# Four regroupings in a one-core hybrid decoder layer: decay rows, a transpose, a weight split and the last products

## The chip, the cores and the metric

The kernel runs on one core of one Trainium2 chip. The metric is device time in microseconds of the whole program, the median of several executions. One execution was also recorded by the hardware profiler; all positions below ("at 995.82") are microseconds from the start of that recording's span. The engines are TensorE (PE: matmuls; PEld: its weight loads), VectorE (DVE), ScalarE (ACT), GpSimd (POOL) and SyncE (SP, which only asks for transfers here). ACT and POOL also ask for transfers; the profile calls the queues SPq, ACTq and POOLq.

## The reference

One decoder layer on 512 tokens of width 1024, all in float32, cut to its steps:

```python
x = x + 0.5 * swiglu(rms_norm(x, norm_ffn1_w), ffn1_w_in, ffn1_w_out)      # D_FF = 2816
x = x + hybrid_mixer(rms_norm(x, norm_mix_w), ...)   # SSD heads beside differential attention
x = x + memory_cross_attention(rms_norm(x, norm_cross_w), rms_norm(mem, norm_mem_w), ...)
x = x + 0.5 * swiglu(rms_norm(x, norm_ffn2_w), ffn2_w_in, ffn2_w_out)
return rms_norm(x, norm_final_w)

def swiglu(h, w_in, w_out):
    gate, up = jnp.split(h @ w_in, 2, axis=-1)
    return (jax.nn.silu(gate) * up) @ w_out

# in hybrid_mixer, for the 16 SSD heads in 4 groups, chunks of 128 tokens:
la_cum = jnp.cumsum(la, axis=2)
seg = la_cum[:, :, :, None] - la_cum[:, :, None, :]
decay = jnp.exp(jnp.where(causal[None, None, :, :, None, None], seg, -jnp.inf))
cb = jnp.einsum('bclgn,bcsgn->bclsg', cc, bc)
y_diag = jnp.einsum('bclsg,bclsgr,bcsgrp->bclgrp', cb, decay, xdt)
...
y_off = jnp.einsum('bclgn,bcgrpn,bclgr->bclgrp', cc, prev, jnp.exp(la_cum))
```

## The kernel before

The activations live as eight tiles `x[0..7]` of 128 channels by 512 tokens. Each weight tile (128 by 1024, 512 KB) is loaded by SP into `wr`, and split into a rounded high part `wh` (ACT, line 153) and a remainder `wl` (DVE, line 154); a product is three matmuls (high by high, low by high, high by low). There are six `wr` buffers and three each of `wh` and `wl`.

The order in which work is written out comes from `Order`: dense generators (the projections, one after the other) and chains (side work such as attention heads) that are resumed when a running estimate of TensorE's time, `od.t`, reaches their due time. SP and POOL execute their instructions in exactly that written order. On PE, ACT and DVE a compiler's planner decides the order from its own estimates of when each instruction will be ready, with what is written earlier going first among ready ones; on the chip each engine then works strictly through the order it was given.

The places that the change touches:

- FFN1 (`ffn1`): a first part with plain projections (`NPLAIN`), then "quads" (`quad`, `add_product`, line 238): blocked products by a scheme with seven products instead of eight, called 11, S1, S2, 12, S3, S4 and 22 by the half-token operands they use. Their operands `s31` and `s24` are sums of token halves of channel pairs, made by `block_sums`. The product 11 goes into the bank `qa`, S1 into `qe`, and `qa` is copied to `qb` by ACT. With `fresh=True` (the first quad of each FFN) the last channel pair is left to the end: `qa` for three pairs, `qe` for three pairs, then the last pair of each. In FFN1 a quad's T1 weight is summed by an accumulating transfer that POOL asks for (line 246).
- SSD groups (`group`): `decays(j)` asks POOL's queue for rows of the cumulative log decay (`cum_d`, in DRAM) for two heads, broadcast over 128 partitions, into the single-buffered tiles `gate` (j=0) and `th` (j=1) (line 820). ACT turns them into decays (lines 879 to 882), DVE masks them (line 883), PE multiplies (`py`); `pf` takes the carried state, `st` (lines 859 to 867).
- `block_sums_in_dram`: a chain that adds weight blocks for FFN2 in DRAM: ACT asks for a copy, POOL four jobs later for the accumulating transfer (line 1143). The list `hold` keeps POOL's part back while a group is between its start and its second half.
- The last projection of cross attention (`out_proj` with `upd_2`) finishes `x[o]` for o = 0..7 and prepares FFN2's operands. `turn` transposes all eight `x` tiles in place through PSUM tiles `pxf` (PE, line 148, then ACT, line 1116), 30 time units after the last one, inside FFN2's first quads.
- FFN2's last output products (`out_blocks` with `last`): `update` adds a PSUM bank to a 128-token row block of `x` (DVE, line 1183), and `final` makes the final norm: a Square with row sum on ACT (1247), `fv` on DVE (1250/1252), the gain on DVE (1253), the power −1/2 on POOL (1258), the scaling of both halves on ACT (1259, 1262; the last half on DVE, 1264), and the stores.

Of the kernel before, what the change touches and what calls it, by code (L numbers as in the profile page):

```python
# [13 lines left out]
AF = mybir.ActivationFunctionType  # L14
# [3 lines left out]
P = 128  # L18
# [80 lines left out]
def body(tc, a, dbg=None):  # L99
# [28 lines left out]
    def acc(s, shape=(P, T)):  # L128
        return acc_p.tile(list(shape), F32, tag="acc", name=nm(s))
# [8 lines left out]
    last, start, last_sum, recent, hold = [], [], [], [], []  # L138
    V, S, G = nc.vector, nc.scalar, nc.gpsimd
    od = Order()  # L140

# [113 lines left out]
    def quad(xs, src, ready, fresh=False):  # L255

        b12, b11, b22, b21 = src[0], src[1], src[2], src[3]
        m1 = raw_w(b11)
        if ready:
            t, t2, m2, m7, m3 = raw_w(ready[0]), raw_w(ready[1]), raw_w(b21), raw_w(b12, b22), raw_w(b22)
            t4 = m2
        else:
            t, m3, m2, m7 = raw_w(b12, b11), raw_w(b22), raw_w(b21), raw_w(b12, b22)
            t2 = t4 = t
        a_ps = acc("qa")  # L270
        e_ps = acc("qe")
        b_ps = acc("qb")
        if fresh:

            n = len(xs)
            w1, w5 = split_w(m1), split_w(t)
            yield from add_product(a_ps, w1, xs, "11", True, range(n - 1))
            yield from add_product(e_ps, w5, xs, S1, True, range(n - 1))
            yield from add_product(a_ps, w1, xs, "11", False, range(n - 1, n))
            S.activation(b_ps, a_ps, AF.Copy)  # L280
            yield from add_product(e_ps, w5, xs, S1, False, range(n - 1, n))
        else:
            yield from add_product(a_ps, split_w(m1), xs, "11", True)
            S.activation(b_ps, a_ps, AF.Copy)
            yield from add_product(e_ps, split_w(t), xs, S1, True)
        p5 = s2("p5")
        S.activation(p5, e_ps, AF.Copy)
        if not ready:
            V.tensor_tensor(t2, t, m3, ALU.add)
        yield from add_product(b_ps, split_w(t2), xs, S2, False)  # L290
        if not ready:
            V.tensor_tensor(t4, t2, m2, ALU.add)
        u2 = s2("u2")
        S.activation(u2, b_ps, AF.Copy)
        V.tensor_tensor(e_ps, e_ps, u2, ALU.subtract)
        yield from add_product(a_ps, split_w(m2), xs, "12", False)
# [180 lines left out]
    def ffn1(h, wa, on_final, at_out):  # L477
        row4, xs = None, []
        wq, plain = iter(a["f1q"]), a["f1i"]
        for ti, (_, nf) in enumerate(THIRDS):  # L480
            g = []
            nq = nf // 2
            if ti == 0:
                for made in ffn_first(h, wa):
                    if made is None:
                        yield
                    else:
                        g.append(split("g", gated(*made, st1.row)))
                row4 = s2("row4")
                V.tensor_scalar(row4, st1.row, 0.25, None, ALU.mult)  # L490
                for n in range(NPLAIN - 2):
                    pg, pu = acc("pg"), acc("pu")
                    yield from proj(pg, load_w(plain[n][0]), h)
                    yield from proj(pu, load_w(plain[n][1]), h)
                    g.append(split("g", gated(pg, pu, st1.row)))
                    xs.append(block_sums(2 * n, C_FFN1, of_halves(h[2 * n], h[2 * n + 1])))
                nq -= NPLAIN // 2
            yield from ffn_quads(xs, wq, st1, nq, whole_tiles(g), BY_TILE, None, ti == 0)
            at_out(ti)
            for o in range(KT):  # L500
# [102 lines left out]
    def steps(pdt):  # L603
# [42 lines left out]
        ct_sb = s2("ct_sb", shape=(64, P))  # L646
        V.tensor_copy(ct_sb, pct)
        nc.gpsimd.dma_start(cum_d, ct_sb)
        dump("cum", cum)


# [145 lines left out]
    def group_dense(g):  # L797
# [6 lines left out]
        for j in range(2):  # L804
            ps = acc("pz")
            yield from proj(ps, load_w(a["wz"][2 * g + j]), h)
            zs.append(silu2(ps))

    def group(g, bt, ct, xs, zs):
        hsl = slice(4 * g, 4 * g + 4)  # L810

        def by_head(t):
            return t.rearrange("p c (h e) -> p c h e", e=64)

        def decays(j):
            rs, both = [], s4(("gate", "th")[j])
            for hh in range(2):
                r = both[:, 2 * hh : 2 * hh + 2].rearrange("p a (b c) -> p (a b) c", c=P)
                hd = 4 * g + 2 * j + hh
                nc.gpsimd.dma_start(r, bass.AP(cum_d.tensor, cum_d.offset + hd * P, [[0, P], [16 * P, 4], [1, P]]))  # L820
                rs.append(r)
            return rs

        hold.append(g)

        pcb = aux("pcb", (P, 4, P))
        for c in range(4):
# [40 lines left out]
            st.append(sc)  # L868
            yield W["gs"] if c < 2 else W["gt"]
        yz = []  # L870
        rs = decays(0)
        for j in range(2):
            py = aux("py")
            e2 = s2("e2")
            for hh in range(2):
# [9 lines left out]
            for c in range(1, 4):  # L885
                mm(pf[:, c * P : (c + 1) * P], st[c - 1][:, j * P : (j + 1) * P], ct[:, c * P : (c + 1) * P], True, True)
            yield W["gd"]
            if j == 1:
                hold.remove(g)
            for c in range(4):  # L890
                for hh in range(2):
                    pp = slice(64 * hh, 64 * hh + 64)
                    mm(py[pp, c * P : (c + 1) * P], xdt[c // 2][:, c % 2, (2 * j + hh) * 64 : (2 * j + hh + 1) * 64], rs[hh][:, c], True, True)
            if j == 0:
                rs = decays(1)
            dsk = dskh[:, 2 * g + j : 2 * g + j + 1]
            V.scalar_tensor_tensor(e2[:, P:], pf[:, P:], 0.5, e2[:, P:], ALU.mult, ALU.mult)
            y = s2("y")
# [209 lines left out]
    def turn():  # L1108

        for n in range(2):  # L1110
            pt = [aux("pxf") for _ in range(4)]
            for tb in range(4):
                for j in range(4):
                    transpose(pt[tb][:, j * P : (j + 1) * P], x[4 * n + j][:, tb * P : (tb + 1) * P])
            for tb in range(4):
                S.activation(x[4 * n + tb], pt[tb], AF.Copy)
                yield 4.0


    isum = [[dram.tile([P, D], F32, name=f"isum{g}{t}") for t in range(2)] for g in range(NF // 2)]  # L1120
# [2 lines left out]
    def block_sums_in_dram():  # L1123
# [22 lines left out]
    def out_blocks(c, g, col4, last):  # L1146

# [34 lines left out]
        def update(tb, half_, src):  # L1182
            V.scalar_tensor_tensor(x[4 * half_ + tb], src, col4[:, tb : tb + 1], x[4 * half_ + tb], ALU.mult, ALU.add)  # L1183
            if last is not None:
                last(tb, half_)

        bank = [acc, aux]
        a_ps = [bank[t]("oa") for t in range(2)]
# [32 lines left out]
        if last is None:  # L1221
# [16 lines left out]
    def ffn2():  # L1238
        wq, in_sums = iter(a["f2q"]), iter(isum)
        col4, gain = None, []  # L1240

        sq = {}

        def final(tb, n):

            xt, ss, junk = x[4 * n + tb], small("fss", 1), s2("junk")
            S.activation(junk, xt, AF.Square, accum_out=ss)
# [6 lines left out]
            if tb not in sq:  # L1254
                sq[tb] = v
                return
            rr = small("frr", 1)
            G.tensor_tensor(rr, v, mhalf[:, 0:1], ALU.pow)  # L1258
            S.activation(x[tb], x[tb], AF.Copy, scale=rr)  # L1259
            nc.sync.dma_start(a["out"][tb][:, :T], x[tb])  # L1260
            if tb < 3:
# [5 lines left out]
        for c, (_, nf) in enumerate(THIRDS):  # L1267
# [10 lines left out]
            yield from out_blocks(c, g, col4, final if at_end else None)  # L1278

    od.add(ffn2())  # L1280
    od.run()
    ctx.close()
# [89 lines left out]
```

## Time and profile before

| | us |
|---|---|
| median of 3 runs | 1337.62 |
| lowest, highest | 1336.28, 1339.88 |
| profiled execution, its time | 1339.54 |
| profiled execution, span from first to last instruction | 1337.8 |
| PE busy | 1310.7 (98%) |
| DVE busy | 975.6 (73%) |
| ACT busy | 667.4 (50%) |
| POOL busy | 129.9 (10%) |
| mean granted TensorE clock | 0.992 |

How to read it: the span is the profiled execution's own; 1.74 us of that execution's time lie around the span. A matmul counts as busy until its modelled end, so that consecutive matmuls overlap and "busy" does not mean that the array is at its peak. "Idle before, releaser" in a row is the time in which that engine did nothing ahead of the instruction, and the event that ended it.

### The profile page before, as it was taken

What the parts mean: (1) busy time and instruction counts of PE and PEld (TensorE: products, weight loads), DVE (VectorE), ACT (ScalarE), POOL (GpSimd) and SP (SyncE); (2) the same over time, 40 slices, a digit from 0 to 9 for tenths busy, and PEclk for the clock granted to TensorE, in tenths of its full rate; (3) what the DMA queues carried; (4) which work ended last, traced back from release to release, by engine and by line L of the source; (5) the groups of instructions that cost most, each with busy time, mean ns of one, the idle gap of its engine ahead of it and who ended that gap; (6) DMA issues with size and microseconds to landing.
All of it is one profiled execution on the core that took longest, in us unless ns stands there. A gap on an engine that the chain in (4) does not pass through costs nothing. (4 is left out here: it accounts for less than half of the span.)

```text
span 1337.8 us, 20033 instructions
## 1 busy us (share of the span) xinstructions
PE 1310.7 (98%) x7769; PEld 1139.7 (85%) x7769; DVE 975.6 (73%) x1535; ACT 667.4 (50%) x1127; POOL 129.9 (10%) x155
## 2 busy tenths in 40 slices
PE   9999999999999999999999999999999999999996
PEld 7888999899887778877778887888889989998995
DVE  6875688477886586557847877656687886887787
ACT  6442455154554465346545546434445654655556
POOL 0000001000020111200112032010002101000000
PEclk9999999999999999999989999999999999999998
DMA  7434577546394636674475557776268977665653
GB/s 269 118 103 126 129 204 237 144 115 190 125 280 125 174 82 106 194 209 111 113 146 154 107 132 220 200 202 160 67 216 210 223 227 208 183 194 183 182 172 118
DMA packets 65695, 222.71 MB, mean 166 GB/s; under 512 B 8424, under 2 KB 10960, under 8 KB 65248
## 3 DMA queue, kind: packets, MB, share of 16 engines
q1 hardware_dynamic: 47088, 150.30, 34.7%
q0 software_dynamic: 14208, 47.79, 20.5%
q10 hardware_dynamic: 4304, 23.33, 5.3%
q8 instruction: 61, 1.00, 0.3%
q14 instruction: 34, 0.28, 0.1%
HBM read 219.24 MB, written 50.91 MB: 202 GB/s over the span
## 5 line engine op out<-in xcount | busy, mean ns | idle before, releaser
L153 ACT ACTIVATE wh<-wr 128x1024 fp32r<-128x1024 f32 (+2 forms) x311 | 317.2, 1022 | 400.9 <-issue 72.9
L154 DVE TENSOR_TENSOR wl<-wr,wh 128x1024 fp32r<-128x1024 f32 (+2 forms) x311 | 366.3, 1178 | 122.0 <-ACT wh L153 120.1
L144 PE MATMUL po<-gh,wh 128*128 128x512 f32 x176 | 68.8, 392 | 0.0
L144 PE MATMUL po<-gl,wh 128*128 128x512 f32 x176 | 68.5, 390 | 0.0
L144 PE MATMUL po<-gh,wl 128*128 128x512 f32 x176 | 68.4, 389 | 0.0
L238 PE MATMUL qa<-hmh,wh 128*128 128x256 f32 x216 | 61.7, 286 | 0.2 <-ACT wh L153 0.2
L238 PE MATMUL qa<-hml,wh 128*128 128x256 f32 x216 | 61.5, 285 | 0.0
L238 PE MATMUL qa<-hmh,wl 128*128 128x256 f32 x216 | 61.4, 284 | 0.0
L144 PE MATMUL pxbc<-hnh,wh 128*128 128x512 f32 x128 | 52.3, 409 | 0.0
L144 PE MATMUL pxbc<-hnh,wl 128*128 128x512 f32 x128 | 50.4, 394 | 0.0
L144 PE MATMUL pxbc<-hnl,wh 128*128 128x512 f32 x128 | 50.1, 391 | 0.0
L238 PE MATMUL qe<-s31h,wh 128*128 128x256 f32 x152 | 43.9, 289 | 4.9 <-ACT s31h L153 3.2
L696 ACT ACTIVATE ec<-ec,mn 128x512 f32<-128x512 f32 (+3 forms) x64 | 35.4, 555 | 26.3 <-DVE mn L695 26.3
L238 PE MATMUL qe<-s31h,wl 128*128 128x256 f32 x152 | 43.6, 287 | 0.8 <-DVE wl L154 0.8
L504 DVE TENSOR_TENSOR upd<-po,row 128x512 f32<-128x512 f32 x24 | 16.6, 690 | 38.1 <-PE po L144 38.0
L238 PE MATMUL qb<-s24h,wh 128*128 128x256 f32 x152 | 43.8, 288 | 0.2
L238 PE MATMUL qb<-s24l,wh 128*128 128x256 f32 x152 | 43.8, 288 | 0.0
L238 PE MATMUL qb<-s24h,wl 128*128 128x256 f32 x152 | 43.8, 288 | 0.0
L238 PE MATMUL qe<-s31l,wh 128*128 128x256 f32 x152 | 43.4, 286 | 0.0
L238 PE MATMUL qe<-s24h,wh 128*128 128x256 f32 x152 | 43.0, 283 | 0.0
L238 PE MATMUL qe<-s24l,wh 128*128 128x256 f32 x152 | 43.0, 283 | 0.0
L238 PE MATMUL qe<-s24h,wl 128*128 128x256 f32 x152 | 43.0, 283 | 0.0
(448 smaller groups left out, 4097.2 us busy)
## 6 DMA issues: line engine op xcount, KB each, us to landing
wr<-in_f2q SPq DMA_DIRECT2D x44, 512.0 KB, 4.4
wr<-in_f1q SPq DMA_DIRECT2D x40, 512.0 KB, 4.2
isum<-in_f2q ACTq DMA_DIRECT2D x22, 512.0 KB, 4.8
wr<-isum SPq DMA_DIRECT2D x22, 512.0 KB, 4.4
wsum<-in_f2b ACTq DMA_DIRECT2D x20, 512.0 KB, 5.5
wr<-wsum SPq DMA_DIRECT2D x20, 512.0 KB, 4.4
wr<-in_f1q POOLq DMA_DIRECT2D x16, 512.0 KB, 6.5
wr<-in_f1o SPq DMA_DIRECT2D x16, 512.0 KB, 3.9
```

Source lines behind the costliest of these rows:

```text
L144: nc.tensor.matmul(out, w, x, start=start, stop=stop)
L153: S.activation(hi, src, AF.Copy),
L154: V.tensor_tensor(lo, src, hi.bitcast(F32), ALU.subtract),
L238: nc.tensor.matmul(out, a_[:, wc], b_, start=first and f == 0 and kp == 0 and j == 0, stop=kp == n - 1 and j == 2, skip_group_check=True)
L504: V.tensor_tensor(upd, po, row4, ALU.mult)
L696: S.activation(ec[:, :n], ec[:, :n], AF.Exp, bias=mn, scale=-1.0, accum_out=sm[c][:, i : i + 1])
```

## The change

Four things are regrouped; nothing is computed differently.

1. FFN1: the block sums of a channel pair are written ahead of that round's two plain projections instead of behind them, and FFN1's first quad is no longer `fresh`. In every quad the T1 weight is split (`w5`) ahead of the copy of `qa` to `qb` in the written order.
2. SSD: `decays(0, j)` is asked for as soon as `cum_d` is written, and `decays(g + 1, j)` directly behind group g's `py` products of the same j. `hold` is gone; the accumulating jobs are 9 instead of 8 time units apart.
3. `turn` is cut in two: tiles 0 to 3 from o = 4 of the last projection on, tiles 4 to 7 between that projection and FFN2. Its 16 transposes each are ordered by source tile.
4. In FFN2's last output products, `final` is cut into `norm` and `store`, and a new function `at_last` writes them out in an order of its own, inside a region in which DVE and ACT keep the written order among the region's instructions.

```diff
 def quad(xs, src, ready, fresh=False):
+        w1, w5 = split_w(m1), split_w(t)
         if fresh:
             n = len(xs)
-            w1, w5 = split_w(m1), split_w(t)
...
         else:
-            yield from add_product(a_ps, split_w(m1), xs, "11", True)
+            yield from add_product(a_ps, w1, xs, "11", True)
             S.activation(b_ps, a_ps, AF.Copy)
-            yield from add_product(e_ps, split_w(t), xs, S1, True)
+            yield from add_product(e_ps, w5, xs, S1, True)
...
 def ffn1(h, wa, on_final, at_out):
                 for n in range(NPLAIN - 2):
+                    xs.append(block_sums(2 * n, C_FFN1, of_halves(h[2 * n], h[2 * n + 1])))
                     pg, pu = acc("pg"), acc("pu")
                     yield from proj(pg, load_w(plain[n][0]), h)
                     yield from proj(pu, load_w(plain[n][1]), h)
                     g.append(split("g", gated(pg, pu, st1.row)))
-                    xs.append(block_sums(2 * n, C_FFN1, of_halves(h[2 * n], h[2 * n + 1])))
...
-            yield from ffn_quads(xs, wq, st1, nq, whole_tiles(g), BY_TILE, None, ti == 0)
+            yield from ffn_quads(xs, wq, st1, nq, whole_tiles(g), BY_TILE)
...
 def steps(pdt):
         nc.gpsimd.dma_start(cum_d, ct_sb)
+        for j in range(2):
+            decays(0, j)
...
+    rows_of = {}
+    def decays(g, j):
+        rows_of[g, j], both = [], s4(("gate", "th")[j])
+        for hh in range(2):
+            r = both[:, 2 * hh : 2 * hh + 2].rearrange("p a (b c) -> p (a b) c", c=P)
+            hd = 4 * g + 2 * j + hh
+            nc.gpsimd.dma_start(r, bass.AP(cum_d.tensor, cum_d.offset + hd * P, [[0, P], [16 * P, 4], [1, P]]))
+            rows_of[g, j].append(r)
...
 def group(g, bt, ct, xs, zs):
-        hold.append(g)
...
-        rs = decays(0)
         for j in range(2):
+            rs = rows_of.pop((g, j))
...
-            if j == 1:
-                hold.remove(g)
             for c in range(4):
                 for hh in range(2):
                     mm(py[...], xdt[...], rs[hh][:, c], True, True)
-            if j == 0:
-                rs = decays(1)
+            if g < 3:
+                decays(g + 1, j)
...
 def upd_2(o, po):
+        if o == 4:
+            od.spawn((0.5 for _ in turn(0)), 1.0)
         if o == KT - 1:
             od.spawn(st_2.finish(8.0), 5.0)
-            od.spawn(turn(), 30.0)
...
+    def turn(n):
+        pt = [aux("pxf") for _ in range(4)]
+        for j in range(4):
             for tb in range(4):
+                transpose(pt[tb][:, j * P : (j + 1) * P], x[4 * n + j][:, tb * P : (tb + 1) * P])
+        for tb in range(4):
+            S.activation(x[4 * n + tb], pt[tb], AF.Copy)
+            yield
...
 def block_sums_in_dram():
-            while hold:
-                yield 1.0
             if n >= LEAD:
                 G.dma_start(to, more, accum_op=ALU.add, max_dma_last_dim=4 * D)
-                yield 8.0
+                yield 9.0
...
 def out_blocks(c, g, col4, last):
-        raws = [[fetch(of, part) for part in parts] for of in (blocks[B22], sums[3])]
-        for n, (ps, which, tb, half_) in enumerate(((e_ps, S4, 0, 1), (b_ps, "22", 2, 0))):
-            ws = [weights(None, part, raw) for part, raw in zip(parts, raws[n])]
-            for t in range(2):
-                for w, part in zip(ws, parts):
-                    yield from some(ps[t], w, which, part, t, False)
-                update(tb + t, half_, ps[t])
+        with tc.manual_schedule(engines={mybir.EngineType.DVE, mybir.EngineType.Activation}):
+            yield from at_last(parts, blocks, sums, e_ps, b_ps, fetch, weights, some, update, last[1])
+
+    def at_last(parts, blocks, sums, e_ps, b_ps, fetch, weights, some, update, store):
+        first, second = parts
+        s4, t4 = ([fetch(of, part) for part in parts] for of in (blocks[B22], sums[3]))
+        ws = [weights(None, part, raw) for part, raw in zip(parts, s4)]
+        wt = [weights(None, first, t4[0])]
+        for w, part in zip(ws, parts):
+            yield from some(e_ps[0], w, S4, part, 0, False)
+        update(0, 1, e_ps[0])
+        yield from some(e_ps[1], ws[0], S4, first, 1, False)
+        wt.append(weights(None, second, t4[1]))
+        yield from some(e_ps[1], ws[1], S4, second, 1, False)
+        store(0)
+        update(1, 1, e_ps[1])
+        for t in range(2):
+            for w, part in zip(wt, parts):
+                yield from some(b_ps[t], w, "22", part, t, False)
+            store(1 + t)
+            update(2 + t, 0, b_ps[t])
+        store(3)
...
 def ffn2():    # final(tb, n) becomes norm(tb, n), which ends with the power, and store(tb):
+            root[tb] = small("frr", 1)
+            G.tensor_tensor(root[tb], v, mhalf[:, 0:1], ALU.pow)
+        def store(tb):
+            rr = root[tb]
             S.activation(x[tb], x[tb], AF.Copy, scale=rr)
             nc.sync.dma_start(a["out"][tb][:, :T], x[tb])
...
+    od.add(turn(1))
     od.add(ffn2())
```

More of the change, by code (lines that the diff above doesn't have):

```diff
@@ L136, in dump @@
             nc.sync.dma_start(dbg[name], t.bitcast(F32) if t.dtype == R32 else t)
-    last, start, last_sum, recent, hold = [], [], [], [], []
+    last, start, last_sum, recent = [], [], [], []
     V, S, G = nc.vector, nc.scalar, nc.gpsimd
@@ L813, in by_head @@
             return t.rearrange("p c (h e) -> p c h e", e=64)
[L815 to L822, printed above, removed]
-        hold.append(g)
         pcb = aux("pcb", (P, 4, P))
@@ L1105, in body @@
     od.add(out_proj(oc, a["wco"], lambda: all(y is not None for y in oc), upd_2))
-    def turn():
-        for n in range(2):
-            pt = [aux("pxf") for _ in range(4)]
+    def turn(n):
+        pt = [aux("pxf") for _ in range(4)]
+        for j in range(4):
             for tb in range(4):
[L1113 to L1117, printed above, removed]
+                transpose(pt[tb][:, j * P : (j + 1) * P], x[4 * n + j][:, tb * P : (tb + 1) * P])
+        for tb in range(4):
+            S.activation(x[4 * n + tb], pt[tb], AF.Copy)
+            yield
     isum = [[dram.tile([P, D], F32, name=f"isum{g}{t}") for t in range(2)] for g in range(NF // 2)]
@@ L1184, in update @@
             if last is not None:
-                last(tb, half_)
+                last[0](tb, half_)
         bank = [acc, aux]
@@ L1240, in ffn2, with norm @@
         col4, gain = None, []
-        sq = {}
-        def final(tb, n):
+        sq, root = {}, {}
+        def norm(tb, n):
             xt, ss, junk = x[4 * n + tb], small("fss", 1), s2("junk")
@@ L1256, in final @@
                 return
-            rr = small("frr", 1)
-            G.tensor_tensor(rr, v, mhalf[:, 0:1], ALU.pow)
+            root[tb] = small("frr", 1)
+            G.tensor_tensor(root[tb], v, mhalf[:, 0:1], ALU.pow)
+        def store(tb):
+            rr = root[tb]
             S.activation(x[tb], x[tb], AF.Copy, scale=rr)
@@ L1277, in ffn2 @@
                     G.dma_start(gain[n], a["final"][n].partition_broadcast(P))
-            yield from out_blocks(c, g, col4, final if at_end else None)
+            yield from out_blocks(c, g, col4, (norm, store) if at_end else None)
+    od.add(turn(1))
     od.add(ffn2())
```

## The prediction

> **What bounds it now.** First the page's busy line: TensorE is the bound, so only what idles or slows TensorE can be won, plus what follows its last matmul.
>
> ```profile
> span 1337.8 us, 20033 instructions
> PE 1310.7 (98%) x7769; PEld 1139.7 (85%) x7769; DVE 975.6 (73%) x1535; ACT 667.4 (50%) x1127; POOL 129.9 (10%) x155
> ```
>
> The other engines' shares say little: 1337.8 − 1310.7 leaves 27.1 us. The second view, TensorE's own waits (total, times, longest), names who ends that idle time:
>
> ```profile
> PE qe L238 <- ACT s31h L153: 3.2, 2, 1.6
> PE py L144 <- DVE gate L883: 2.5, 2, 2.2
> PE pf L144 <- DVE st L867: 1.9, 2, 1.0
> PE qe L238 <- ACT wh L153: 1.7, 1, 1.7
> ```
>
> Each belongs to a place that the change touches. I placed them in the timeline and asked for busy time by stretch (stretch, length, PE busy and count, PEld, DVE, ACT, POOL, granted clock, DMA share, GB/s):
>
> ```profile
> 78.25:80.95 2.70, 1.00 (x7) 0.65 (x5) 2.67 (x5) 2.57 (x4) 0.00 (x0) 1.00 0.00 0
> 80.95:84.36 3.41, 3.41 (x19) 3.41 (x18) 1.32 (x3) 1.50 (x3) 0.00 (x0) 0.51 0.46 154
> 270.40:279.72 9.32, 6.68 (x50) 6.26 (x51) 6.46 (x6) 5.04 (x7) 0.00 (x0) 1.00 0.01 2
> 692.48:696.85 4.37, 1.59 (x7) 1.04 (x7) 3.22 (x7) 4.37 (x13) 0.00 (x0) 0.83 0.77 133
> 696.85:702.12 5.27, 5.27 (x15) 4.11 (x14) 2.36 (x5) 0.37 (x2) 0.00 (x0) 0.50 0.78 214
> 802.92:808.00 5.08, 2.59 (x23) 1.83 (x23) 2.90 (x6) 4.79 (x11) 0.92 (x1) 1.00 1.03 161
> 995.82:998.97 3.15, 1.44 (x10) 1.08 (x9) 2.27 (x4) 2.61 (x4) 0.00 (x0) 1.00 0.00 0
> 998.97:1002.38 3.41, 3.41 (x19) 3.41 (x18) 2.88 (x4) 2.06 (x3) 0.00 (x0) 0.53 0.37 114
> ```
>
> Read the clock column beside the idle time. Two stretches with 1.7 us idle (2.70 − 1.00; 3.15 − 1.44) are each followed by 3.41 us at half clock, and the one at 692 by more than 5 us. TensorE is busy there and yet does half its work: a stall is paid twice. The stretches at 270 and 802 idle as long and keep the full clock.
>
> **FFN1's first quad (78.25 to 84.36).** Idle 1.70 plus half of 3.41 makes 3.4 us. It waits for the sums of the last channel pair:
>
> ```profile
> 29.00:73.20 44.20, 44.20 (x195) 36.35 (x194) 34.99 (x56) 18.00 (x25) 1.96 (x2) 1.00 0.38 101
> 77.20 0.42 DVE L205 TENSOR_TENSOR s<-fe,fo 128x256 f32<-128x256 f32 x1
> 79.34 0.61 ACT L153 ACTIVATE s31h<-s 128x512 fp32r<-128x512 f32 x1
> ```
>
> Written a round (two projections) earlier, these sums need only `x`, there since the start. The work is the same; DVE has 9.2 us free of 44.2 beforehand (44.20 − 34.99), and the sums leave one round for the one before. So the wait goes: −3.4. Worst: a first weight split gets behind the first sums, and up to 3.4 comes back; I take nothing, since TensorE is fully fed for 44 us. Dropping `fresh` costs nothing then: same matmuls, and the `qa` copy lies beside the whole S1 product.
>
> **FFN2's first quad (995.82 to 1002.38).** Same pattern, 1.71 plus 1.7: 3.4 us.
>
> ```profile
> 994.84 0.42 DVE L205 TENSOR_TENSOR s<-fe,fo 128x256 f32<-128x256 f32 x1
> 995.96 1.06 ACT L153 ACTIVATE wh<-wr 128x1024 fp32r<-128x1024 f32 x1 [3.48 <-PE qa L238]
> 996.92 0.61 ACT L153 ACTIVATE s31h<-s 128x512 fp32r<-128x512 f32 x1
> 1019.06 0.87 PE pxf L148 x8
> ```
>
> `s31` is ready at 995.26, but ACT's queue holds a weight split ahead of it that waits for `qa`'s end. The second `turn` puts 16 transposes, 16 × 0.87/8 = 1.7 us, ahead of the quad, taken from inside FFN2, so net nothing on TensorE. They move `qa`'s end to about 997.6; the planner then has 1.7 us more to put `s31h` first, and its split (0.61, then DVE's half) is done near 997. If it keeps the weight split first, the wait moves along and nothing is won. The 3.48 us in which ACT idled hold `turn`'s four copies; tile 7 is due in the last quarter of the transposes only. Both ends 0 and 3.4; nearest is the row of 3.48 idle, so −3.0 with 0.4 left. The first `turn`'s 16 transposes are as neutral: its tiles are final by o = 4.
>
> **Decay rows (692.48 to 702.12, 802.92 to 808).** Idle and half clock: 4.37 − 1.59 = 2.8 plus half of 5.27 = 2.6, so 5.4 us; and 5.08 − 2.59 = 2.5 us.
>
> ```profile
> 674.17 1.88 POOL L820 DMA_DIRECT2D gate<-cum_d  x2
> 691.59 0.63 ACT L879 ACTIVATE e<-gate 64x512 f32<-64x512 f32 x1 [4.32 <-DMA gate<-cum_d]
> 693.55 0.49 PE L144 MATMUL pf<-th,st 128*128 128x128 f32 x2 [0.91 <-ACT st L859]
> 803.18 0.63 ACT L879 ACTIVATE e<-gate 64x512 f32<-64x512 f32 x1 [2.07 <-DMA gate<-cum_d]
> 805.24 0.43 PE L144 MATMUL py<-gate,xdt 128*64 128x128 f32 x2 [2.17 <-DVE gate L883]
> th<-cum_d POOLq DMA_DIRECT2D x8, 256.0 KB, 17.3
> POOL ysq L912 <- ACT ysq L910: 137.7, 4, 41.5
> ```
>
> The rows asked for at 674.17 land some 17 us later; ACT, strictly in order, stands 4.32 us before them with the copy of `st` queued behind, and that stops `pf`. At 803 the same wait delays `gate` itself. Asked for a group ahead, they get most of the distance between two groups (803.18 − 674.17 is two of them, so some 60 us each; I count on 40) against a median landing of 17.3. So −5.4 and −2.5. The 16 requests stay 16. What is new on POOL's queue: `decays(g + 1, j)` waits until group g's `py` has freed the one buffer, and accumulations and the group's `ysq` addition stand behind it. POOL already waits 137.7 us in four groups for `ysq`, later than `py`, so 0. Group 0's requests wait in the queue for `cum_d` to land, long before a group needs them: 0. Without `hold`, accumulating transfers run beside the groups; see the rivals.
>
> **T1 split ahead of the copy (270.40 to 279.72).** 9.32 − 6.68 = 2.6 us are idle here.
>
> ```profile
> 250.40 0.92 POOL L246 DMA_DIRECT2D wr<-in_f1q  x1
> wr<-in_f1q POOLq DMA_DIRECT2D x16, 512.0 KB, 6.5
> 270.19 0.58 ACT L284 ACTIVATE qb<-qa 128x512 f32<-128x512 f32 x1 [12.92 <-PE qa L238]
> 270.95 1.06 ACT L153 ACTIVATE wh<-wr 128x1024 fp32r<-128x1024 f32 x1
> ```
>
> T1 lands near 257 (250.40 + 6.5) and could be split in ACT's 12.92 idle us, but the copy was queued first. The planner takes what is ready by its own reckoning, so ACT's idle queue tells that it held T1 for unready until `qa`'s end; writing the split earlier doesn't alter that. Ends 0 and −2.6; I take 0 and keep the rest as a rival.
>
> **The tail.** The last matmul ends at 1326.78 + 0.39 = 1327.17; the span goes on to 1337.8.
>
> ```profile
> 1320.66 0.39 PE L1173 MATMUL oe<-wl,s24h 128*128 128x512 f32 x1
> 1322.69 0.74 DVE L1183 SCALAR_TENSOR_TENSOR x<-oe,col,x 128x512 f32<-128x512 f32 x1
> 1326.78 0.39 PE L1173 MATMUL ob<-wl,gh 128*128 128x512 f32 x1
> 1329.63 0.61 ACT L1247 ACTIVATE junk<-x 128x512 f32<-128x512 f32 x1
> 1331.57 0.72 ACT L1262 ACTIVATE x<-x,frr 128x512 f32<-128x512 f32 x1 [0.62 <-POOL frr L1258]
> 1332.19 0.71 ACT L1259 ACTIVATE x<-x,frr 128x512 f32<-128x512 f32 x1
> 1332.81 0.70 ACT L1259 ACTIVATE x<-x,frr 128x512 f32<-128x512 f32 x1
> DMA to landing us min/median/max: 2.0/2.2/3.0
> ```
>
> In the new order ACT runs Square, then waits for `fv` and the power, then scales two halves, before the next block's Square. One block costs 1331.57 − 1329.63 = 1.94, plus two scalings at 0.62 (1332.19 − 1331.57), 3.18 us; TensorE delivers a block in 9 products, 2.0 us. So this chain of four, not TensorE, sets the end. It starts when the fifth tile is updated: at the earliest 1321.05 (1320.66 + 0.39) + 0.1 + 0.77, that is 1321.9; if DVE is as late as now, 1322.69 + 0.77 = 1323.5. The last scaling ends 3 × 3.18 + 1.94 + 0.70 = 12.2 later, at 1334.1 to 1335.7, against 1332.81 + 0.70 = 1333.5 now: +0.6 to +2.2. The last stores no longer queue behind others, so they land in 2.0 to 2.2 instead of 3.0, some 0.9 back. Tail: −0.3 to +1.3, taken +0.5. A late split of T4's second part may stop TensorE shortly; the vector chain ends later anyhow.
>
> **Sum.** −3.4 − 3.0 − 5.4 − 2.5 + 0 + 0.5 = −13.8, against 1339.54 of the profiled execution: 1325.7. The median lies 1.9 below that execution, so 1323.8; I say 1324.
>
> [...]
>
> **Rivals.**
> - Only stalls go, the half-clock stretches have another cause: 1.7 + 1.7 + 2.6 us stay, so 1330. Against it: three such stretches, each directly behind a wait. For it: 270 and 802 idle alike and keep the clock. 6%.
> - The change doesn't do what it says in FFN2: the planner keeps the weight split ahead of `s31h`. 3.0 stay, with a fresh wait of like size 6: 1327 to 1330. 10%.
> - T1's split does come first: 2.6 more, 1321. For it: landed 13 us early. 22%.
> - Slower: without `hold` the accumulations fall into the groups, where the DMA share is already 0.77 to 1.03, and weights land late. A weight that comes 1.7 us late with its half-clock stretch costs 3.4; four such waits undo the gain to 1324 + 13.6, near no change, and from six on it is slower, 1344. Against it: TensorE's waits name no transfer now. 6% slower, 6% about even.
>
> **Chances.** The forecast 50%, with T1 22%, quad 10%, clock 6%, transfers 12%. Faster by over 0.3% (4 us, about what this measurement tells from no change): 0.88. Same 0.06, slower 0.06. The range goes down to the T1 case with no rest in FFN2 and the best tail (1321 − 0.4 − 0.8, less the 1 to 2 us by which the runs before differ: 1317), and up to the clock and quad rivals with the worst tail (1330 + 0.8, and the same spread: 1332); it leaves out the transfers.
>
> **What would show it.** After: no TensorE wait on `s31h` near 80 or 996; no half clock between the first microseconds and the end; no ACT wait on `gate` or `th` transfers; `pf` and `py` waits under 0.5; ACT's Squares at the end 3.2 apart. Wrong if a new TensorE wait on `wh`, `wl` or a transfer stands in the trace, above all from 520 to 840, or the last Square begins later than 1333 less the gain.

## The result and the profile after

The change made the kernel slower: 1349.28 us (median of 6, 1347.24 to 1355.57) against 1338.18 for the kernel before on the same chip, a ratio of 1.009 (95% interval 1.0066 to 1.0114). The forecast was 1324. First the page's head, then TensorE's waits (total, times, longest):

```profile
span 1346.4 us, 20042 instructions
PE 1312.3 (97%) x7769; PEld 1140.0 (85%) x7769; DVE 973.4 (72%) x1535; ACT 669.0 (50%) x1127; POOL 131.1 (10%) x155
...
PE pf L144 <- ACT st L862: 5.3, 1, 5.3
PE pt L148 <- DVE mn L697: 2.6, 1, 2.6
```

The waits on `s31h` and `gate` are gone. Two new ones stand at the top, and the chain of work that ended last (start, length, what) has a transfer in it at both places:

```profile
439.64 17.47 DMA bias<-rel_z
...
785.56 13.41 DMA wsum<-in_f2b
```

The stretches that the forecast spoke of, and the two new ones (stretch, length, PE busy, PEld, DVE, ACT, POOL, granted clock, DMA share, GB/s):

```profile
75.00:83.00 8.00, 8.00 (x69) 8.00 (x68) 6.04 (x7) 4.93 (x7) 0.00 (x0) 1.00 0.28 77
268.00:274.00 6.00, 4.38 (x24) 4.18 (x24) 3.94 (x4) 2.81 (x3) 0.00 (x0) 0.72 0.00 0
456.00:460.00 4.00, 1.83 (x10) 0.97 (x8) 1.71 (x7) 2.02 (x6) 0.00 (x0) 1.00 0.40 105
460.00:468.00 8.00, 6.13 (x20) 4.44 (x20) 7.25 (x20) 4.91 (x12) 0.00 (x0) 0.57 0.54 146
686.00:698.00 12.00, 12.00 (x64) 10.20 (x63) 7.42 (x14) 6.66 (x17) 0.00 (x0) 1.00 0.56 182
794.00:801.00 7.00, 1.68 (x7) 1.10 (x7) 0.63 (x2) 1.17 (x3) 1.09 (x2) 0.83 0.85 242
801.00:809.00 8.00, 6.56 (x19) 5.12 (x19) 7.97 (x14) 6.53 (x14) 0.00 (x0) 0.51 0.22 63
988.00:1003.00 15.00, 15.00 (x79) 12.77 (x78) 11.43 (x19) 7.71 (x12) 0.00 (x0) 1.00 0.56 190
```

At 75, 686 and 988 TensorE is full and at full clock (1.00), as forecast. At 456 and 794 it stands, and then runs at half clock (0.57 from 460, 0.51 from 801). To see what each place is worth, take the start of the same matmul in both traces and subtract; the difference of this lag across a place is its cost:

| place (time before) | forecast | measured |
|---|---|---|
| FFN1's first quad (70 to 90) | −3.4 | −3.7 |
| T1 (262 to 285) | 0 | +0.7 |
| head 1's scores (440 to 475) | 0 | +7.1 |
| 475 to 510 | – | +1.4 |
| decay rows, group 2 (680 to 710) | −5.4 | −6.3 |
| decay rows, group 3 (780 to 815) | −2.5 | +7.9 |
| FFN2's first quad (960 to 1050) | −3.0 | −2.1 |
| behind TensorE's end | +0.5 | +2.2 |
| all the rest | 0 | +1.2 |
| sum | −13.8 | +8.4; the spans differ by 8.6 |

The first loss in rows: GpSimd's queue, then the first VectorE instruction that needs the bias, then TensorE.

```profile
425.60 1.56 POOL L819 DMA_DIRECT2D gate<-cum_d  x2 [2.41 <-DMA cum_d<-ct_sb]
427.15 1.49 POOL L819 DMA_DIRECT2D th<-cum_d  x2
439.64 0.88 POOL L676 DMA_DIRECT2D bias<-rel_z  x1
457.25 0.69 DVE L697 CUSTOM_DVE_ANT_0 ec<-ps,bias 128x512 f32<-128x512 f32 x1 [9.26 <-DMA bias<-rel_z]
461.87 0.47 PE L148 MATMUL pt<-ident,ec 128*128 128x128 f32 x1 [2.64 <-DVE mn L697]
```

Group 0's rows are asked for from 425.60; the bias, asked for at 439.64, is there at 457. The second loss:

```profile
785.56 0.93 POOL L1142 DMA_DIRECT2D wsum<-in_f2b  x1
786.20 0.89 POOL L936 DMA_DIRECT2D mem<-in_memT  x1
791.51 0.93 POOL L1142 DMA_DIRECT2D wsum<-in_f2b  x1
799.83 0.51 ACT L157 ACTIVATE hm<-mem,par 128x256 fp32r<-128x256 f32 x1 [10.35 <-DMA mem<-in_memT]
800.25 0.36 ACT L862 ACTIVATE st<-pst 128x256 f32<-128x256 f32 x1
800.66 0.79 PE L144 MATMUL pf<-th,st 128*128 128x128 f32 x2 [5.32 <-ACT st L862]
```

With `hold` gone, accumulations go out among the tiles of the second memory pass. ScalarE, in order, waits 10.35 us for a tile, with `st`'s copy behind it, and `pf` waits for `st`. DMA share in this stretch: 0.85.

### The profile page after: what moved, and what is told of

Same layout as the page of the kernel before. It is cut to its first block, busy times and chain, and to the rows that moved or that the text cites. A ratio compares the mean times of both kernels' runs of the same rounds, so it can differ in the third digit from the quotient of the medians.

```text
span 1346.4 us, 20042 instructions
## 1 busy us (share of the span) xinstructions
PE 1312.3 (97%) x7769; PEld 1140.0 (85%) x7769; DVE 973.4 (72%) x1535; ACT 669.0 (50%) x1127; POOL 131.1 (10%) x155
## 4 chain that ended last, share of the span: by engine, by line
PE 71%; issue 18%; DMA 4%; DVE 3%; POOL 2%; ACT 1%; POOLq 0%; SPq 0%; ACTq 0%; DVEq 0%
PE qb L238 10%; PE po L144 7%; PE qa L238 7%; PE qe L238 7%; PE pxbc L144 6%; PE pm L144 6%; PE pcq L144 3%; PE ob L1172 3%; PE pz L144 2%; PE oa L1172 2%; PE oe L1172 2%; PE pa L144 2%; PE pv L144 2%; PE pg L144 2%; PE pu L144 2%
## 5 line engine op out<-in xcount | busy, mean ns | idle before, releaser
L238 PE MATMUL qb<-s31h,wl 128*128 128x256 f32 x152 | 43.0, 283 | 0.0
L238 PE MATMUL qb<-hmh,wh 128*128 128x256 f32 x152 | 43.0, 283 | 0.0
```

What stands on the lines that cost most here:

```text
L238: nc.tensor.matmul(out, a_[:, wc], b_, start=first and f == 0 and kp == 0 and j == 0, stop=kp == n - 1 and j == 2, skip_group_check=True)
```

## Experiments

Ratios below are to the kernel before, run beside each (medians 1336.4 to 1338.5 us); kernels of different experiments are compared by them.

**e1: group 0's rows later.**

```diff
-        for j in range(2):      # behind cum_d's store
-            decays(0, j)
+        if g == 0:              # head of group_dense(0)
+            for j in range(2):
+                decays(0, j)
```

> The changed kernel, with group 0's four decay requests moved ten places down GpSimd's queue, behind the three bias requests and to the head of group 0's dense work. Nothing else moves: the instruction orders of TensorE, VectorE, ScalarE and SyncE are those of the changed kernel. Theory A (the four row transfers stand ahead of an accumulation and a bias on one software queue, the bias lands some 15 us late, and the wait of head 1's scores at 458 with the half-clock window behind it is theirs): that bias lands in 3 to 8 us, the 7.1 us lost at 458 to 468 are gone, 1342 us (1340 to 1344). Rival B (the bias is late because the transfer engines are full at that place whoever asks, share 0.99 there): the wait stays within 1.5 us, 1349. Rival C (the rows are merely late somewhere else: group 0's own decay work now waits for them near 500): the 7.1 go and 2 to 5 come back, 1345 to 1347.

1341.04 us, 1.0027 (1.0015 to 1.004). Across 440 to 475 the lag doesn't change any more (−2.14 to −2.15): the whole 7.1 is gone. Transfers asked for from 425 to 475 (KB each, median us to landing), after and then e1:

```profile
wr<-in_wxbc SPq DMA_DIRECT2D x3, 512.0 KB, 20.6
...
bias<-rel_z POOLq DMA_DIRECT2D x3, 256.0 KB, 17.5
gate<-cum_d POOLq DMA_DIRECT2D x2, 256.0 KB, 11.0
th<-cum_d POOLq DMA_DIRECT2D x2, 256.0 KB, 16.5
```

```profile
wr<-in_wxbc SPq DMA_DIRECT2D x3, 512.0 KB, 4.1
...
bias<-rel_z POOLq DMA_DIRECT2D x3, 256.0 KB, 6.4
```

The rows are the cause. From 425.6 to 439 (columns as above), after and then e1, the transfer engines move about as many bytes, and are busy for 0.85 of the time with the rows, 0.38 without:

```profile
425.60:439.00 13.40, 13.40 (x66) 11.23 (x66) 5.29 (x7) 6.48 (x15) 4.04 (x6) 1.00 0.85 113
```

```profile
425.60:439.00 13.40, 13.40 (x67) 11.22 (x65) 5.29 (x7) 6.48 (x15) 0.72 (x1) 1.00 0.38 119
```

But the weights on SyncE's queue were late with the bias, so theory A's "one queue" is not shown by this; e13 and e14 take it up.

**e2, e3, e4: the hold, near the memory tiles only, and in full.** e2 holds the accumulations from the start of the second memory pass to its end; e3 is e2 with e1's edit; e4 is e1's edit and the old hold:

```diff
+        hold.append(g)          # e4: start of group(g)
+            if j == 1:          # e4: behind pf of the second pair
+                hold.remove(g)
+            while hold:         # e2, e3, e4: ahead of each accumulation
+                yield 1.0
```

> The changed kernel, with the accumulating requests of the block sums held back only while the eight tiles of the second memory pass are being asked for (from the start of that pass to its last split), nowhere else. Theory A (accumulations among the memory tiles on GpSimd's software queue make the tiles late, their splits stand ahead of group 3's first state copy on ScalarE, and TensorE waits for that copy at 795 to 801 and then runs in a half-clock window): the 5.3 and 1.4 us waits go and with them the window, in all 8 to 9.5 us, 1340.5 us (1339 to 1343). Rival B (the missing hold costs in all four groups, not here): under 2 us here, 1347 to 1349. Rival C (the tiles are late because group 3's decay rows, asked a group ahead, stand in the queue too): the wait is halved at most, 1345 to 1348.

> Both of the edits of the two kernels before it. If the two losses are two places of one mechanism and nothing else is lost: the sum of both gains, 1333 us (1330 to 1336), below the 1338 of the kernel before. If removing one only shifts the other stretch onto another place of the half-clock grid: 1336 to 1342.

> The changed kernel with group 0's decay requests late as in the first, and with the old hold put back in full (no accumulation is asked for from the start of a group to its second head pair's products, in each of the four groups). Theory A with hold needed only near the memory tiles: as the third kernel, 1333 us within 2. If accumulations cost inside every group: 2 to 4 us less, 1329 to 1331. If holding them pushes the sums towards their use in the second FFN: 2 to 6 us more, 1335 to 1339, with waits for transfers of wsum or isum on SyncE's weight loads after 1000 us.

e2: 1346.25, 1.0072 (1.0049 to 1.0094), not told apart from the change. e3: 1338.8, 1.0014 (1.0003 to 1.0025). e4: 1332.73, 0.9966 (0.9953 to 0.9978), the first that is faster than before. Theory A's place is right (from 780 to 815 the lag grows by 6.6 us in e1 and falls by 0.8 in e4) and its reach too short: in e3 an accumulation still goes out 0.64 us ahead of the first tile, and ScalarE still waits 8.88 us for one, after 10.4 in e1. First e3, then e4:

```profile
778.06 0.94 POOL L1149 DMA_DIRECT2D wsum<-in_f2b  x1
778.70 0.90 POOL L937 DMA_DIRECT2D mem<-in_memT  x1
790.87 0.51 ACT L157 ACTIVATE hm<-mem,par 128x256 fp32r<-128x256 f32 x1 [8.88 <-DMA mem<-in_memT]
```

```profile
779.07 0.63 POOL L940 DMA_DIRECT2D mem<-in_memT  x1
787.44 0.51 ACT L157 ACTIVATE hm<-mem,par 128x256 fp32r<-128x256 f32 x1 [4.45 <-DMA mem<-in_memT]
```

In e4 waits of 1.4 and 1.0 us are left there, without half clock. Group 3's rows, now asked for ahead of the tiles, are the likely rest of the 4.45; that was not tried apart.

**e15: the hold put back alone, rows early.**

```diff
 the edit of e4 without that of e1
```

> The changed kernel with the old hold put back and nothing else; group 0's rows early. If the two losses are independent: 1332.7 and the 8.2 that the late rows saved, 1341 (1339 to 1343), with the wait at 458 and without the one at 795. If the hold also clears the queue at 425 to 457, or the losses share a half-clock window: 1333 to 1338.

1340.86, 1.0031 (1.0017 to 1.0046). Early rows cost 0.0065 with the hold (e15 less e4) and 0.0063 without (the change less e1): two losses, and independent. The profiled execution has the wait at 458 again (4.28 and 2.25 us).

**e5: the kernel before without its hold.**

```diff
-            while hold:
-                yield 1.0
```

> The kernel before with one thing taken from it: the accumulating requests are no longer held back inside the four groups; the decay rows are still asked inside the group, the rest is as before. Theory A (holding the accumulations is what keeps the transfers on GpSimd's queue in time, wherever the rows are asked): the 256 KB row requests and the memory tiles now stand behind 512 KB accumulations, the waits near 692 and 790 to 820 grow, in all 8 to 20 us slower, 1345 to 1357. Rival B (the hold is needed only because the rows are asked a group ahead): within 3 us of before, 1334 to 1340.

1363.86, 1.0191 (1.017 to 1.0213): the largest effect of all, beyond the range of theory A, and rival B is out. Asked inside the group, the rows themselves are late; ScalarE waits 24.9 us in all for `gate`'s rows, 7.6 before. TensorE's waits:

```profile
PE pf L144 <- ACT st L859: 8.0, 3, 3.3
...
PE py L144 <- DVE th L883: 4.7, 2, 3.6
PE py L144 <- DVE gate L883: 4.3, 1, 4.3
```

With the rows asked for a group ahead most of this price is gone: without the hold 8 us are left (e1 to e4), at the memory tiles.

**e13, e14: queue, bytes or pieces?** e13 asks for the biases on ScalarE's queue, rows where the change has them. e14 is e1, with four other 256 KB loads in the rows' old place, in pieces (contiguous runs) of 2 KB in place of 512 bytes; they are not used.

```diff
-        nc.gpsimd.dma_start(bias, ...)                    # e13
+        nc.scalar.dma_start(bias, ...)
+        for n in ("gate", "th"):                          # e14, behind cum_d's store
+            both = s4(n).rearrange("p a b -> p (a b)")
+            for hh in range(2):
+                hs = slice(hh * T, (hh + 1) * T)
+                nc.gpsimd.dma_start(both[:, hs], a["f2q"][0][0][:, hs])
```

> The changed kernel with the eight bias requests on ScalarE's queue in place of GpSimd's; group 0's rows stay where the change has them, and nothing is held back. Theory A (order within one software queue: the bias waits behind rows and accumulations): the bias lands in 3 to 8 us, the 7.1 us at 458 go, 1342 (1340 to 1344). Theory B (the transfer engines are shared, and the rows fill them whichever queue the others use; the weight loads on SyncE's queue were late too): the bias lands in 12 us or more, the wait at 458 stays above 1.5 us, 1346 to 1351.

> The changed kernel with group 0's rows late (1341.0), and at the place in GpSimd's queue where the change has them four other requests of the same 256 KB each, into the same buffers, of 2 KB in a row instead of 512 bytes; what they bring is not used. Theory A (the bytes and the place in the queue cost): as the change, wait at 458 back, 1346 to 1350. Theory B (the small packets of the rows cost, 512 bytes each): they land in 6 us or less, no wait at 458, 1341 (1339.5 to 1343).

e13: 1345.23, 1.0071 (1.0047 to 1.0095); the decisive bias, asked for by ScalarE at 438.44, still stops VectorE until 455.25:

```profile
438.44 0.33 ACTq L676 DMA_DIRECT2D bias<-rel_z  x1
455.25 0.69 DVE L697 CUSTOM_DVE_ANT_0 ec<-ps,bias 128x512 f32<-128x512 f32 x1 [8.20 <-DMA bias<-rel_z]
```

That is 16.8 us on another queue, and 5.1 of the 7.1 us stay (440 to 473). ScalarE's own copy of a weight block (`isum`), asked for at 430.67, took 19.9 us there, 4.0 in e1. e14: 1338.1, 1.0011 (0.9997 to 1.0026), no wait at 458. Its transfers asked for from 420 to 475:

```profile
bias<-rel_z POOLq DMA_DIRECT2D x3, 256.0 KB, 6.0
gate<-in_f2q POOLq DMA_DIRECT2D x2, 256.0 KB, 4.1
th<-in_f2q POOLq DMA_DIRECT2D x2, 256.0 KB, 4.3
```

Theory B both times, each time a little faster than its range. As many bytes from the same place in the same queue cost nothing. They need not wait for `cum_d` and go out 0.6 us behind its request, the rows 3.0; but they had landed by 428, 10 us ahead of the bias's request. So the rows cost because they are cut into 512 bytes, or because all 128 partitions read the same 32 KB, which was not told apart; the profile's packets don't help, for in this stretch of the changed kernel none lies between 512 bytes and 2 KB. What the rows fill holds up all three queues: GpSimd's bias took 17.5 us (6.4 in e1) and SyncE's loads 20.6 (4.1 in e1) in the changed kernel, ScalarE's bias 16.8 in e13. 256 KB in pieces of 512 bytes took 11.0 to 16.5 us (the changed kernel) and in pieces of 2 KB 4.1 to 4.3 (e14). The two loads differ in their source too, so this doesn't settle whether the piece is to blame.

**e9, e12: the memory tiles on SyncE's queue**, without hold (on e1) and with it (on e10).

```diff
-            mk = mem[k] if early else memory_tile(k, G)
+            mk = mem[k] if early else memory_tile(k, nc.sync)
```

> The changed kernel with group 0's rows late (1341.0) and, this time without any hold, the eight memory tiles of the second pass asked for on SyncE's queue, among the weight loads, in place of GpSimd's. Same bytes, same accumulations. Theory A (the tiles are late because they stand behind rows and accumulations on one software queue): the wait of 5.4 us for group 3's first state copy and the half-clock window behind it go, 7 to 9 us less, 1333 (1331.5 to 1335). Rival B (the transfer engines are full at that place, and any queue waits): the tiles land as late or make the weights behind them late, 1339 to 1345.

> The tenth kernel with the memory tiles on SyncE's queue as in the ninth, the hold kept. Theory A: the two waits left at 790 (1.4 and 1.0 us for VectorE's states, behind a split that waits 4.5 us for a tile) go, 1.5 to 2.4 us less than the tenth. Rival B (the tiles now stand among the weight loads, which come later for it): no gain, or up to 2 us lost at 795 to 830.

e9: 1336.29, 0.9995 (0.9982 to 1.0007), between its theories: the 5.4 us wait is gone, but the tiles took 12.9 us (median) here too, after 11.3 in e1, and came in time because SyncE's queue runs ahead: it asked for the first at 733, and ScalarE used it at 789. New waits of 1.9 (`ndiag`) and 1.8 us (`gate`) take part back. e12: 1328.86, 0.9936 against e10's 0.993: rival B.

**e7, e10: T1.** e7 puts the copy of `qa` behind T1's split; e10 (on e6, below) also the copy of the memory statistics' row, whose matmuls it writes 20 in place of 6 time units behind the sums that they take; its expectation leaves that out. e11, e12 and e16 have it too.

```diff
+            with behind(hi5):                              # e7, e10; hi5: T1's split on ScalarE
                 S.activation(b_ps, a_ps, AF.Copy)
+            with behind(halves_of[:1] if self.n == MEM else []):     # e10, in Stat.finish; the same split
                 S.activation(self.row, pr, AF.Copy)
-        yield from st_mem.finish(6.0)                      # e10
+        yield from st_mem.finish(20.0)
```

> The same kernel with one instruction of ScalarE moved: in the first FFN's second quad the split of the second product's weights (T1) is issued ahead of the copy of the first product's sum; the orders of all other engines are the same. Theory A (the weights have landed some 5 us before, and the split waits only behind the copy, which waits for the whole first product): the two waits of 1.67 and 0.76 us at 269 go, and the half-clock window behind them (1.0 us) with them, 2.4 to 3.4 us less, 1329.8 (1329 to 1330.5). Rival B (the split waits for the accumulated weights' landing): no change, 1332.7.

> The kernel with late rows, hold and the old end (0.9942 of before), with two instructions of ScalarE behind the split of T1: the copy of the first product's sum, and the copy of the memory row, which the run with only the first moved showed standing ahead of the split too. Theory A (T1 waits for these two copies and for nothing else): both waits at 269 go, 2.2 to 2.4 us less, and no half-clock window there in any execution (up to 1 us more), 0.992 of before, some 1327 (1326 to 1328). Rival B (the weights of T1 land late): at most 0.5 us less.

e7: 1331.81, 0.9956 (0.9938 to 0.9973), within e4's interval; theory A falls as put. ScalarE's queue in e7, and then in e10:

```profile
267.08 0.38 ACT L394 ACTIVATE row<-nrow 128x256 f32<-128x256 f32 x1 [13.15 <-PE nrow L145]
267.37 1.05 ACT L154 ACTIVATE wh<-wr 128x1024 fp32r<-128x1024 f32 x1
268.31 0.59 ACT L287 ACTIVATE qb<-qa 128x512 f32<-128x512 f32 x1
```

```profile
258.82 1.06 ACT L154 ACTIVATE wh<-wr 128x1024 fp32r<-128x1024 f32 x1 [4.38 <-PE po L145]
267.36 0.58 ACT L287 ACTIVATE qb<-qa 128x512 f32<-128x512 f32 x1 [7.48 <-PE qa L239]
```

A second instruction, the row's copy, had held the split for 13.15 us. With both behind it the split runs 8.5 us earlier and the two waits are gone: −3.2 us at 269 beside e6. The median gained less: 1327.81, 0.993 (0.9915 to 0.9944) against e6's 0.9942, some 1.6 us, and the intervals overlap; in the profiled execution 2.4 us came back at 790, around the waits for `st`, and its mean granted clock is 0.996, as in e6's, with 1.00 at T1 (268 to 274).

**e6, e8, e11: the end.** e6 is e4 with the old last products; e8 has everything of the end in a written order, with the additions and Squares ahead of the scalings; e11 is e10 with the two last Squares ahead of all scalings but block 0's, and with the second halves of blocks 1 and 2 scaled on VectorE, as block 3's was.

```diff
+            if tb:                            # e11; before: if tb == 3
+                V.tensor_scalar(x[4 + tb], x[4 + tb], rr, None, ALU.mult)
...
+            late.append((tb, rr))
+            if tb in (1, 2):                  # leave the scaling for later
+                return
+            with behind([square.ins] if tb else []):
+                for tb, rr in late:
+                    S.activation(x[tb], x[tb], AF.Copy, scale=rr)
```

> The kernel with group 0's rows late and the hold put back (1332.7), with the last products and their norms written as in the kernel before, in the scheduler's own order. Theory A (in program order each of the last four Squares stands behind the scalings of the row block ahead of it, so the four blocks' chains run one after the other, 3.2 us each, and the work behind TensorE's end grew from 10.6 to 12.8 us): 2.2 us less, 1330.5 (1329.5 to 1331.5), TensorE's end to the span's end 10.4 to 10.8. Rival B (the old order only moves the same waits ahead of TensorE's end): TensorE's end later by as much, 1332.7 within 0.8.

> The same kernel with the end in another order: the additions into the last four row blocks and their Squares are issued ahead of the scalings of the blocks before (ScalarE: Squares of x4, x5, x2, then block 0's scaling, Square of x3, then the other scalings), the second halves' scalings on VectorE, two gain products on GpSimd, and the last weights' splits ahead of the additions. Theory A (the end is a chain of four turns through ScalarE, VectorE and GpSimd, serial only by the order in which ScalarE is given its work): the last scaling ends some 5 us after TensorE's end instead of 9.5, 4 to 5 us less, 1328 (1327 to 1329.5). Rival B (VectorE's updates of the last products set the end, whatever the order): as the old tail, 1330.5 to 1332.

> The same, with the end's last two Squares ahead of all scalings but block 0's, and the second halves' scalings of blocks 1 to 3 on VectorE. Theory A (ScalarE's seven scalings between the Squares are what is left behind TensorE's end in the old order): the last scaling 1.7 us earlier, 1325.3 beside 1327 (1324.5 to 1326). Rival B (VectorE's gain products and GpSimd's powers set it): within 0.5 of the one before.

e6: 1329.52, 0.9942 (0.9927 to 0.9958), so the new end cost 0.0024, some 3 us; from TensorE's last matmul to the end 10.6 us beside 12.8 in e4: theory A. e8: 1333.38, 0.9963 (0.9949 to 0.9977), no better than e4: neither theory as put. My order made VectorE's splits of the last weights wait for Squares, and of the VectorE instructions beside its two products on GpSimd one took 1.35 us in place of 0.69:

```profile
1320.60 1.28 POOL L1293 TENSOR_TENSOR x<-x,gain 128x512 f32<-128x512 f32 x1 [3.30 <-ACT junk L1290]
1321.07 1.35 DVE L154 TENSOR_TENSOR wl<-wr,wh 128x512 fp32r<-128x512 f32 x1 [1.31 <-ACT wh L153]
```

e11: **1326.19 us, 0.9918 (0.9903 to 0.9932)**, the fastest median of the study, 1.6 us below e10, run beside it. From TensorE's last matmul to the end it is 9.7 us, 0.9 less than in e6 and e10: theory A's direction, and half of its 1.7.

**e16: e11 with the old turn.**

```diff
-            od.spawn((0.5 for _ in turn(0)), 1.0)          # at o == 4
+            od.spawn(turn(), 30.0)                         # behind st_2.finish, as before
```

> The best kernel so far (0.9918 of before) with the turn around the second FFN's start as in the kernel before: sixteen transposes twice from inside the FFN, not around the last projection's end. The changed kernel's trace put the turn's worth at 2.0 us where the forecast had 3.0. Theory A (worth 2.0 to 2.4: the wait on s31h and its half-clock window gone, new waits of 0.3 to 0.7 us at three places): 2.0 us slower than the eleventh kernel, 0.9933 of before, 1328.2 (1327 to 1329.5). Rival B (the forecast's 3.0 is there and the difference is the executions'): 1329.2 or more.

1326.44, 0.9929 (0.991 to 0.9949): not told apart from e11, but not from theory A's 0.9933 either. The traces decide. Across the FFN's start (960 to 1050) the lag falls by 2.7 us with the old turn and by 2.6 with the new, and the wait on `s31h` doesn't come back. So the mechanism of theory A is not there in this kernel, nor is rival B's 3.0.

## Why the prediction was wrong, step by step

- **The clock and FFN1.** Right: −3.7 for −3.4, full clock at 75 to 83. Its size has luck in it: e5, with FFN1 as before, has the same stall (1.60 us for `s31h`) and keeps the full clock from 80.95 to 84.36, and loses 1.5 us less there than the trace that the forecast was read from. Group 2's rows: −6.3 for −5.4, right.
- **"Group 0's requests wait in the queue for `cum_d` to land, long before a group needs them: 0."** This step failed, with 7.1 us. It asked who needs the rows and what stands behind them in GpSimd's instruction order. It did not ask which transfers run beside them: the four row requests of 256 KB keep the shared engines at 0.85 for 13 us, where e1 has 0.38, and the biases of the next heads are due behind that (e1, e13, e14). The row of 17.3 us to landing, quoted in the prediction, was the warning.
- **Missing `hold`.** This step failed too. The sum has nothing for it; the prediction priced it as a rival, by late weights, and gave it 12%: "TensorE's waits name no transfer now". That was the state with the hold. e5 shows what the hold was worth, 1.9%, and e4 what its absence costs the changed kernel, 8 us, at one place, near 795: what holds TensorE up is no weight but a state copy, which stands behind the late memory tiles in ScalarE's order. Group 3's −2.5 could not show there.
- **FFN2's first quad.** −2.1 for −3.0, and nothing shows the turn as the cause (e16). In e5, where only the hold was taken away, the lag falls by 2.1 us at the same place with the old turn, for ScalarE's order has `s31h` ahead of the weight split:

```profile
1022.66 0.63 ACT L153 ACTIVATE s31h<-s 128x512 fp32r<-128x512 f32 x1 [2.80 <-DVE s L205]
1023.32 1.06 ACT L153 ACTIVATE wh<-wr 128x1024 fp32r<-128x1024 f32 x1
```

  The planner made this order from an edit to requests alone; why it did is not shown.
- **T1.** The 0 was right: the split's place in the program changes nothing, as argued. What held it was not the copy alone, as the prediction read it (e7), but two copies (e10), and the stall of 2.4 us, at full clock before, has a half-clock stretch in this trace (0.72 from 268 to 274), +0.7.
- **The end.** Spacing of the blocks right: 3.18 forecast, 3.18 between the Squares at 1337.04 and 1340.22; the chain's start was sized wrong. Its first Square begins at 1330.60, that is 1324.2 in the time before (TensorE's lag there is 6.4), where I had 1321.9 to 1323.5:

```profile
1329.96 0.63 ACT L1261 ACTIVATE junk<-x 128x512 f32<-128x512 f32 x1 [2.99 <-DVE x L1182]
1330.60 0.62 ACT L1261 ACTIVATE junk<-x 128x512 f32<-128x512 f32 x1
...
1337.04 0.61 ACT L1261 ACTIVATE junk<-x 128x512 f32<-128x512 f32 x1
...
1340.22 0.61 ACT L1261 ACTIVATE junk<-x 128x512 f32<-128x512 f32 x1
```

  A Square of another block stood ahead of it and waited 2.99 us for VectorE. Cost: +2.2 for +0.5.
- **Left open.** The 1.4 us lost from 475 to 510 are in every kernel built on the changed one and not in e5; nothing was tried on them. So is the rest of 1.2. The accumulating jobs' new spacing, 9 in place of 8, was not undone alone.

## What to carry to other kernels

Before a request is moved earlier, look at what is asked for in the window it moves into, on every queue, and at the DMA share and the time to landing of requests of its kind: their bytes alone don't say how long they keep the engines from the others (256 KB took 4.1 to 4.3 us in e14, 11.0 to 16.5 in the changed kernel). A line that only holds something back has a price that the profile with it can't show; take it away alone and measure. And an edit that makes the planner reorder ScalarE can earn its gain somewhere it was never aimed at: undo it alone before you credit it.

## Not expected of the hardware

- 256 KB in pieces of 512 bytes out of one 32 KB tile took 11.0 to 16.5 us, and in pieces of 2 KB out of a weight block 4.1 to 4.3 (the changed kernel and e14); beside the first, 512 KB loads on another queue took 20.6 us in place of 4.1 (the changed kernel and e1).
- The same stall at T1, 1.67 and 0.76 us, cost a half-clock stretch in some traces and none in others: from 268 to 274 the granted clock is 0.72 after (quoted above), and 1.00 in e2, in the kernel before (to 279.72) and, here, in e13:

```profile
268.00:274.00 6.00, 4.35 (x31) 3.93 (x32) 4.14 (x4) 3.39 (x5) 0.00 (x0) 1.00 0.00 0
```

  The half-clock stretches inside the traces before and after last one, two or three times 3.41 us: 3.41, 6.83 and 3.41 us before (from 80.99, 695.39 and 999.18), 3.41, 6.83 and 10.24 after (from 269.61, 460.75 and 798.67). In each trace they begin whole multiples of 3.41 us apart.
- A VectorE split of 512 columns took 1.35 us beside a GpSimd product (e8), and 0.69 without one (before, at 1319.03).
